# Feed-forward down projection as seven block products, in a two-layer Conformer trunk on one core

## The chip, the core and the metric

The kernel runs on one NeuronCore of a Trainium2 chip. The core has five engines with queues of their own: PE (TensorE, matrix products into PSUM), DVE (VectorE, elementwise), ACT (ScalarE, elementwise with tables), POOL (GpSimd) and SP (SyncE, which issues most DMAs). Each engine runs its own list of instructions strictly in order, and waits on semaphores for the others. The metric is the time in microseconds of one execution on the device; lower is better.

## The reference

Two layers. Each layer is a half-step feed-forward network, a mixer (a causal convolution group beside a differential attention group), and a second half-step feed-forward network. The activations are 512 positions by 1024 channels in float32, the hidden width is 2816.

```
def swiglu(h, w_gate, w_up, w_down):
    return (jax.nn.silu(h @ w_gate) * (h @ w_up)) @ w_down

for l in range(DEPTH):                                   # DEPTH = 2
    x = x + 0.5 * swiglu(rms_norm(x, ffn1_norm[l]), ffn1_w_gate[l], ffn1_w_up[l], ffn1_w_down[l])
    h = rms_norm(x, mix_norm[l])
    a, g, q, k, v = jnp.split(h @ w_in[l], splits, axis=-1)
    conv_out = conv_module(a, g, conv_w[l], conv_b[l], conv_norm[l])
    ...                                                  # q, k normed per head, lambda, diff_out
    x = x + jnp.concatenate([conv_out, diff_out], axis=-1) @ w_out[l]
    x = x + 0.5 * swiglu(rms_norm(x, ffn2_norm[l]), ffn2_w_gate[l], ffn2_w_up[l], ffn2_w_down[l])
```

## The kernel before

**Layout.** Channels lie on the 128 partitions: x is eight tiles of 128 channels by 512 positions, the hidden layer is 22 tiles ("features" below) of 128. A product is formed in three matmuls, because each float32 operand is split in two float32r parts, hi and lo: hi times hi, hi times lo, lo times hi (`mm3`). Weights are split on the fly: SP loads a raw tile, ACT copies it to hi, DVE subtracts hi from raw and gets lo (`parts_of`, L96 and L97; in the mixer POOL does the subtraction). The raw, hi and lo tiles lie in rings (`RING`): five raw, four hi and four lo of 1024 columns, and two each of 512.

**Feed-forward (`ffn`).** The 22 features are done in three parts (`PARTS`) of 6, 8 and 8. In the first part the gate and up products are plain: eight channel tiles, 512 positions wide, 48 matmuls a feature. In the two later parts gate and up of one feature are computed together by a Strassen-Winograd scheme (`seven`): the contraction is cut in two halves, the positions in two halves, and gate and up are the two block columns, so that seven block products of half width (256 positions) take the place of eight. `Halves` makes the sums of the normed activations (th, tl) that it needs; `sums` makes the sums of the weights: an accumulating DMA on POOL's queue adds u1 to two operands at once (L137), and two POOL additions make two more (L142, L143). The seven products of a feature are 84 matmuls of 128 by 256 columns (L362). The seventh product is deferred: it is issued in the next feature, behind its first two products (`before()`, `rest`), and followed by the multiplication with Silu of the gate and the split of the hidden tile into hi and lo (`gated`, L401 and L402).

After the features of a part its down product is done plainly: for each of the eight output tiles, `gather` loads the weights, and 3 matmuls a feature, 512 wide, add up in one PSUM bank (ps_d, L159, L162, L163); DVE adds half of it to x (L452). After the last part this loop also calls `after(m)`: the tile of the next norm (`Prep.tile`), or the store of the output.

**Mixer.** It starts with products of its own (`conv_in`, `project`), with the row statistics placed inside the first ones (`first_products` with `early`). The bias of the attention is made once, in the first feed-forward network (`aside`: `make_bias`, then `make_scalars`): small DMAs and a broadcast of 1280 KB in POOL's queue, and two matmuls on PE.

**Order.** The framework orders each engine's list by a cost model of its own at build time, except for matmuls that are held in program order (`keep_in_program_order`). All weight loads are on SP's queue. An instruction that waits holds whatever stands behind it on its engine.

Of the kernel before, what the change touches and what calls it, by code (L numbers as in the profile page):

```python
# [39 lines left out]
STATS_AT = 5  # L40
HS = SEQ // 2


PARTS = ((0, 6), (6, 8), (14, 8))
PLAIN = PARTS[0][1]

SPACE = 392
# [19 lines left out]
def trunk(ctx: ExitStack, tc: tile.TileContext, xt, par, lamv, relb, onehot,  # L67
# [21 lines left out]
    RING = {"wraw": 5, "whi": 4, "wlo": 4, "wraw2": 2, "whi2": 2, "wlo2": 2}  # L89

    def ring(tag, n=1024):
        dt = F32 if "raw" in tag else F32R
        return wp.tile([P, n], dt, tag=tag, name=tag, bufs=RING[tag])

    def parts_of(raw, hi, lo, eng=None):
        S.activation(hi, raw, AF.Copy)  # L96
        (eng or V).tensor_tensor(out=lo, in0=raw, in1=f32(hi), op=ALU.subtract)  # L97

    def chunk(src, eng=None):
        raw, hi, lo = ring("wraw"), ring("whi"), ring("wlo")  # L100
        nc.sync.dma_start(raw, src)
        parts_of(raw, hi, lo, eng)
        return hi, lo

    def gather(src, blocks, eng=None):

        raw, hi, lo = ring("wraw"), ring("whi"), ring("wlo")
# [8 lines left out]
        c = slice(0, len(blocks) * P)  # L116
        parts_of(raw[:, c], hi[:, c], lo[:, c], eng)
        return hi, lo

    def sums(g, u):  # L120

        h = slice(0, 512), slice(512, 1024)
        w = {}

        def give(name, t, n, raw):
            w[name] = tuple(p[:, h[n]] for p in t)
            parts_of(raw, *w[name])

        whole = ring("wraw")
        nc.sync.dma_start(whole, g)  # L130
        two = ring("wraw")
        nc.sync.dma_start(two[:, h[0]], g[:, h[0]])
        nc.sync.dma_start(two[:, h[1]], u[:, h[1]])
        u2 = ring("wraw2", 512)
        nc.sync.dma_start(u2, u[:, h[1]])

        nc.gpsimd.dma_start(  # L137
            two.rearrange("p (b c) -> p b c", b=2), u[:, h[0]].unsqueeze(1).broadcast_to([P, 2, 512]), accum_op=ALU.add
        )

        more = ring("wraw")
        G.tensor_tensor(more[:, h[0]], two[:, h[1]], whole[:, h[0]], op=ALU.add)  # L142
        G.tensor_tensor(more[:, h[1]], more[:, h[0]], whole[:, h[1]], op=ALU.add)  # L143
        t = ring("whi"), ring("wlo")
        parts_of(whole, *t)
        for n, name in enumerate(("g1", "g2")):
            w[name] = tuple(p[:, h[n]] for p in t)
        t = ring("whi"), ring("wlo")
        give("u2u1", t, 0, two[:, h[1]])
        give("g1u2u1", t, 1, more[:, h[0]])  # L150
        give("u2", (ring("whi2", 512), ring("wlo2", 512)), 0, u2)
        t = ring("whi"), ring("wlo")
        give("all", t, 0, more[:, h[1]])
        give("g1u1", t, 1, two[:, h[0]])
        return w
# [21 lines left out]
    lead = [[ring("wraw"), ring("whi"), ring("wlo")] for _ in range(4)]  # L177
    for half in range(2):
        h, kk = slice(half * 512, (half + 1) * 512), range(half * KT // 2, (half + 1) * KT // 2)
        nc.sync.dma_start(x[:, kk[0], :], xt[kk[0]])  # L180
        for n, (raw, hi, lo) in enumerate(lead):
            nc.sync.dma_start(raw[:, h], gu1[0, n // 2, n % 2][:, h])
            parts_of(raw[:, h], hi[:, h], lo[:, h])
        for k in kk[1:]:
            nc.sync.dma_start(x[:, k, :], xt[k])
    lead = [[tuple(t[1:]) for t in lead[2 * m : 2 * m + 2]] for m in range(2)]
    ident = const.tile([P, P], F32, tag="ident", name="ident")
    make_identity(nc, ident)
    ones = const.tile([P, P], F32, tag="ones", name="ones")
    G.memset(ones, 1.0)  # L190
    ones_r = const.tile([P, P + SPACE], F32R, tag="ones_r", name="ones_r")[:, :P]
    V.tensor_scalar(ones_r, ones, 1.0, None, op0=ALU.mult)
# [72 lines left out]
    def wpart(w, b, n=P):  # L265
        return w[0][:, b * n : (b + 1) * n], w[1][:, b * n : (b + 1) * n]

# [13 lines left out]
    def first_products(pr, w, ps, early=False):  # L281
# [5 lines left out]
        for k in range(KT):  # L287
            if early and k == STATS_AT:
                rc, v = rows_rstd(pr.s, DM, pin=True)
            for i in range(2):  # L290
                mm3(ps[0][i], wpart(w[0][i], k), pr[k], k == 0, k == KT - 1, pin=early and k in (0, STATS_AT))
        for i in range(2):
            for k in range(KT):
                if early and i == 0 and k == STATS_AT:
                    r = spread(rc, "rb", pin=True)
                mm3(ps[1][i], wpart(w[1][i], k), pr[k], k == 0, k == KT - 1, pin=early and k in (0, STATS_AT))
        return rc, v, r

    def pair_banks(turn):
        tag = ("sc", "po", "mm")[turn % 3]  # L300
# [3 lines left out]
    class Halves:  # L304
# [4 lines left out]
        def __init__(self, fp, pr, r):  # L309
# [4 lines left out]
            free = [(fp, tag, 1) for tag in ("hh6", "hh7", "hl6", "hl7")]  # L314
            free += [(wp, tag, 2) for tag in ("whi2", "wlo2") for _ in range(2)]
            a, b = slice(0, HS), slice(HS, SEQ)
            for j in range(KT // 2):
                for k in (j, j + KT // 2):
                    pool, tag, bufs = free.pop()
                    h = pool.tile([P, SEQ], F32, tag=tag, name="hn", bufs=bufs)  # L320
# [3 lines left out]
                t = fp.tile([P, 3, HS], F32, tag="ht", name="ht", bufs=2)  # L324
# [20 lines left out]
    def seven(halves, w, banks, fp, before, last):  # L345
# [9 lines left out]
        def go(ps, wt, xt, first=False):  # L355
# [3 lines left out]
            for j in range(KT // 2):  # L359
                (wh, wl), (xh, xl) = wpart(w[wt], j), at(j)  # L360
# [21 lines left out]
        def rest():  # L382
# [4 lines left out]
            V.scalar_tensor_tensor(us, us, -1.0, g, op0=ALU.mult, op1=ALU.mult)  # L387
            return banks[0]
# [3 lines left out]
    def ffn(pr, gu, dn, after, lead=None, aside=None):  # L392
        with tc.tile_pool(name="ffn", bufs=1) as fp:
            r = halves = None
            for m0, many in PARTS:
                hh, held, late = [], [], []

                def gated(n, us):
                    hi = fp.tile([P, SEQ], F32R, tag=f"hh{n}", name="hh")
                    lo = fp.tile([P, SEQ], F32R, tag=f"hl{n}", name="hl")  # L400
                    S.activation(hi, us, AF.Copy)  # L401
                    V.tensor_tensor(lo, us, f32(hi), op=ALU.subtract)  # L402
                    hh.append((hi, lo))

                def finish():
                    if late:
                        n, rest = late.pop()
                        gated(n, rest())

                for mm in range(many):  # L410
                    m = m0 + mm
                    if m == 4 and aside:
                        aside()
                    if m >= PLAIN:
                        w = sums(gu[m, 0], gu[m, 1])
                        late.append((mm, seven(halves, w, pair_banks(m), fp, finish, mm == many - 1)))
                        continue
                    w = lead[m] if lead and m < 2 else [chunk(gu[m, 0]), chunk(gu[m, 1])]
                    held.append((mm, w, pair_banks(m)))
                    if m == 0:  # L420
                        continue
                    if m == 1:
                        first = lead_products if lead else first_products
                        _, _, r = first(pr, [h[1] for h in held], [h[2] for h in held])
                    else:
                        for i in range(2):
                            products(pr, w, held[-1][2][i], i)
                    for n, _, ps in held:
# [6 lines left out]
                        gated(n, us)  # L435
# [3 lines left out]
                finish()  # L439
                if m0 == 0:  # L440
                    halves.settle()
                blocks = [divmod(m0 + kk, HALF) for kk in range(many)]
                blocks = [(half, m * HALF + f) for m in range(KT) for half, f in blocks]
                w = None
                for m in range(KT):
                    ps = bank("mm", "ps_d")
                    for kk in range(many):
                        b = m * many + kk
                        if b % 8 == 0:
                            w = gather(dn, blocks[b : b + 8])  # L450
                        mm3(ps, wpart(w, b % 8), hh[kk], kk == 0, kk == many - 1)
                    V.scalar_tensor_tensor(x[:, m, :], ps, 0.5, x[:, m, :], op0=ALU.mult, op1=ALU.add)  # L452
                    if m0 + many == FT:
                        after(m)


    bias = const.tile([P, HEADS, SEQ], F32, tag="bias", name="bias")

    def make_bias():
# [15 lines left out]
        nc.gpsimd.dma_start(bias, skew)  # L475
# [38 lines left out]
    def mixer(l, pr, after):  # L514
        with tc.tile_pool(name="mix", bufs=1) as mp, tc.tile_pool(name="mt", bufs=2) as mt:
            us = [None] * CT
            row = {}
            turn = iter(range(12))
# [383 lines left out]
```

## Time and profile before

| | |
|---|---|
| median of 3 runs | 1822.91 us (1822.59 to 1823.46) |
| profiled execution | 1822.3 us span, which is its own time from the first to the last instruction; the page gives no other for it |
| PE, DVE, ACT, POOL busy | 1794.2, 1201.3, 886.2, 623.2 us |
| granted TensorE clock | 0.997 of full on average |
| DMA | 227.01 MB, 125 GB/s on average |

The profile gives the busy time of each engine, groups of instructions by line, the chain of work that ended last (each step followed back to what released it), and what an engine waited for. Matmul times in it overlap their neighbours, so the distance from one start to the next is what a matmul costs. L numbers are lines of the kernel; a name such as `wlo<-wraw,whi` is output and inputs of an instruction, with buffer numbers left out; "[8.84 <-DMA lamv]" is the engine's idle time before an instruction and what ended it.

### The profile page before, as it was taken

Reading aid. Unit: us, or ns where it says so; the run is one execution under the profiler, and the core shown is the slowest. Engines: PE = TensorE matmul, PEld = TensorE weight load, DVE = VectorE, ACT = ScalarE, POOL = GpSimd, SP = SyncE. Lnnn points to the kernel's source line nnn. Section 1 sums busy time; section 2 is a strip of 40 time slices with the busy share of each in tenths; the row PEclk is TensorE's granted clock in tenths of the full one; section 3 lists DMA queues with packets and bytes.
Section 4 is the critical chain, followed back from the end, with each engine's and each line's share of the span. In section 5 each row is a group of like instructions: output and inputs, shape, how many; then the busy total and the mean of one; then the engine's idle time right before and its main releaser. Section 6 shows DMA issues by size and latency. Waiting matters only on the chain.

```text
span 1822.3 us, 27888 instructions
## 1 busy us (share of the span) xinstructions
PE 1794.2 (98%) x10692; PEld 1586.2 (87%) x10692; DVE 1201.3 (66%) x1854; ACT 886.2 (49%) x1452; POOL 623.2 (34%) x431
## 2 busy tenths in 40 slices
PE   8899999999999999999999999999999999999999
PEld 6779999888779889999888998998887888998997
DVE  6757547558876857647567574665688588574662
ACT  5536436445764436436434463554458444363551
POOL 3024024149943023124110241322698420231320
PEclk9999999999999999999999999999999999999999
DMA  6346546422213347546423564563231123564561
GB/s 225 128 99 191 150 129 178 134 92 83 81 35 94 98 105 191 149 126 184 132 90 108 133 175 132 151 185 99 77 99 64 47 94 113 134 175 133 151 173 48
DMA packets 105238, 227.01 MB, mean 125 GB/s; under 512 B 11559, under 2 KB 29238, under 8 KB 105104
## 3 DMA queue, kind: packets, MB, share of 16 engines
q1 hardware_dynamic: 85824, 188.78, 31.9%
q0 software_dynamic: 18992, 36.28, 11.6%
q8 instruction: 84, 1.38, 0.3%
q14 instruction: 50, 0.41, 0.1%
q10 hardware_dynamic: 288, 0.16, 0.0%
HBM read 223.07 MB, written 3.42 MB: 124 GB/s over the span
## 4 chain that ended last, share of the span: by engine, by line
PE 92%; DVE 4%; DMA 1%; issue 1%; ACT 1%; DVEq 0%; ACTq 0%
PE ps_pair L362 35%; PE ps_d L159 9%; PE ps_d L162 9%; PE ps_d L163 9%; PE ps_pair L163 5%; PE ps_pair L162 5%; PE ps_pair L159 5%; PE ps_pair L570 2%; PE ps_pair L569 2%; PE ps_pair L571 2%; PE ps_out L159 1%; PE ps_out L162 1%; PE ps_sc L687 1%; PE ps_out L163 1%; DMA lamv<-in_lamv 1%
## 5 line engine op out<-in xcount | busy, mean ns | idle before, releaser
L96 ACT ACTIVATE whi<-wraw 128x512 fp32r<-128x512 f32 (+1 forms) x580 | 458.8, 815 | 670.5 <-PE ps_d L162 231.4
L97 DVE TENSOR_TENSOR wlo<-wraw,whi 128x512 fp32r<-128x512 f32 (+1 forms) x536 | 509.0, 972 | 208.5 <-ACT whi L96 204.0
L362 PE MATMUL ps_pair<-acth,wlo 128*128 128x256 f32 x1024 | 289.8, 283 | 0.0
L362 PE MATMUL ps_pair<-actl,whi 128*128 128x256 f32 x1024 | 289.8, 283 | 0.0
L362 PE MATMUL ps_pair<-acth,whi 128*128 128x256 f32 x1024 | 289.7, 283 | 0.0
L159 PE MATMUL ps_d<-hh,whi 128*128 128x512 f32 x704 | 274.5, 394 | 8.9 <-DVE x L452 3.6
L162 PE MATMUL ps_d<-hl,whi 128*128 128x512 f32 x704 | 275.7, 392 | 1.5 <-DVE hl L402 1.5
L163 PE MATMUL ps_d<-hh,wlo 128*128 128x512 f32 x704 | 274.6, 391 | 0.0
L137 POOL DMA_DIRECT2D wraw<-in_gu x64 | 77.0, 1203 | 491.1 <-DMA wraw<-in_gu 197.6
L362 PE MATMUL ps_pair<-th,wlo 128*128 128x256 f32 x768 | 217.3, 283 | 0.0
L362 PE MATMUL ps_pair<-tl,whi 128*128 128x256 f32 x768 | 217.2, 283 | 0.0
L362 PE MATMUL ps_pair<-th,whi 128*128 128x256 f32 x768 | 217.2, 283 | 0.0
L159 PE MATMUL ps_pair<-acth,whi 128*128 128x512 f32 x512 | 200.6, 395 | 5.8 <-ACT whi L96 5.8
L162 PE MATMUL ps_pair<-actl,whi 128*128 128x512 f32 x512 | 201.1, 393 | 0.3
L163 PE MATMUL ps_pair<-acth,wlo 128*128 128x512 f32 x512 | 200.3, 392 | 0.7 <-DVE wlo L97 0.7
L362 PEld LDWEIGHTS ps_pair<-actl,whi 128*128 128x128 f32 x1024 | 196.6, 192 | 0.3
L362 PEld LDWEIGHTS ps_pair<-acth,whi 128*128 128x128 f32 x1024 | 196.6, 192 | 0.3
L362 PEld LDWEIGHTS ps_pair<-acth,wlo 128*128 128x128 f32 x1024 | 196.6, 192 | 0.0
L452 DVE SCALAR_TENSOR_TENSOR x<-ps_d,x 128x512 f32<-128x512 f32 x96 | 65.3, 690 | 196.0 <-PE ps_d L163 195.9
L142 POOL TENSOR_TENSOR wraw<-wraw 128x512 f32<-128x512 f32 x64 | 91.0, 1423 | 294.1 <-DMA wraw<-in_gu 253.2
L159 PEld LDWEIGHTS ps_d<-hh,whi 128*128 128x128 f32 x704 | 132.8, 189 | 42.2 <-DVE x L452 9.0
L162 PEld LDWEIGHTS ps_d<-hl,whi 128*128 128x128 f32 x704 | 132.9, 189 | 28.6 <-DVE hl L402 2.0
(173 smaller groups left out, 3311.5 us busy)
## 6 DMA issues: line engine op xcount, KB each, us to landing
wraw<-in_gu SPq DMA_DIRECT2D x108, 512.0 KB, 3.6
wraw<-in_gu SPq DMA_DIRECT2D x200, 256.0 KB, 3.7
wraw<-in_gu POOLq DMA_DIRECT2D x64, 512.0 KB, 5.5
wraw<-in_wqkv SPq DMA_DIRECT2D x24, 512.0 KB, 3.5
wraw<-in_dn SPq DMA_DIRECT2D x52, 192.0 KB, 2.9
wraw<-in_wag SPq DMA_DIRECT2D x16, 512.0 KB, 3.6
wraw<-in_wout SPq DMA_DIRECT2D x16, 512.0 KB, 3.4
wraw<-in_dn SPq DMA_DIRECT2D x24, 320.0 KB, 3.5
```

Source lines behind the costliest of these rows:

```text
L96: S.activation(hi, raw, AF.Copy)
L97: (eng or V).tensor_tensor(out=lo, in0=raw, in1=f32(hi), op=ALU.subtract)
L137: nc.gpsimd.dma_start(two.rearrange("p (b c) -> p b c", b=2), u[:, h[0]].unsqueeze(1).broadcast_to([P, 2, 512]), accum_op=ALU.add)
L142: G.tensor_tensor(more[:, h[0]], two[:, h[1]], whole[:, h[0]], op=ALU.add)
L159: first = T.matmul(ps, wh, xh, start=start, stop=False)
L162: T.matmul(ps, wh, xl, start=False, stop=False)
L163: T.matmul(ps, wl, xh, start=False, stop=stop)
L362: mm = T.matmul(ps, l, r, start=first and i == j == 0, stop=False, skip_group_check=True)
L452: V.scalar_tensor_tensor(x[:, m, :], ps, 0.5, x[:, m, :], op0=ALU.mult, op1=ALU.add)
L569: T.matmul(ps[n], xh[:, t], wh, start=k == 0, stop=False)
L570: T.matmul(ps[n], xh[:, t], wl, start=False, stop=False)
L571: T.matmul(ps[n], xl[:, t], wh, start=False, stop=k == KT - 1)
```

## The change

- Both later parts also do their down product as seven half-width block products. The part's eight features are two groups of four, the output tiles are taken in pairs m and m + 4, and each of the four pairs is one block (`seven_down`). `Hidden` makes the sums of the hidden tiles that this needs (in the buffers yh, yl), `down_sums` those of the weights. The order of the features in a part is changed so that the groups' weights lie in runs.
- The seventh product of a block is deferred into the next block, of the last block of a part into the next part, and of the last part into the first products of the next stage (`tail`, `begin`, `ORDER`); at the end of the kernel it stands alone.
- `sums` is written anew for both uses: each of the seven operands is a raw tile of 512 columns, taken in the order of use; u1 is added by separate accumulating DMAs to two of them, and the two further sums are done on DVE where POOL did them.
- All weight rings have nine tiles of 512 columns.
- `aside` calls make_scalars ahead of make_bias; the bias tile lies in the mixer's pool and is loaded from DRAM in each mixer. The last tap of the convolution writes to SBUF where an ACT copy did. `pair_banks` counts through the whole kernel. The plain down of the first part uses these banks too.

```
-PARTS = ((0, 6), (6, 8), (14, 8))
+PARTS = (
+    ((0, 1, 2, 3, 4, 5), "first"),
+    ((6, 11, 7, 12, 8, 13, 9, 14), "seven"),
+    ((10, 18, 15, 19, 16, 20, 17, 21), "last"),
+)
+ORDER = (0, 4, 1, 5, 2, 6, 3, 7)
...
-    RING = {"wraw": 5, "whi": 4, "wlo": 4, "wraw2": 2, "whi2": 2, "wlo2": 2}
+    RING = {"wraw": 9, "whi": 9, "wlo": 9}
...
+    def sums(load, n=512):
+        def get(part, dst, add=False):
+            for to, src in load(part):
+                if add:
+                    nc.gpsimd.dma_start(dst[:, to], src, accum_op=ALU.add)
+                else:
+                    nc.sync.dma_start(dst[:, to], src)
+        w = {}
+        r = {k: ring("wraw", n) for k in ("u2u1", "u2", "g1", "g2", "all", "g1u2u1", "g1u1")}
+        get("u2", r["u2u1"])
+        get("g1", r["g1u1"])
+        get("u1", r["u2u1"], True)
+        get("u2", r["u2"])
+        get("g1", r["g1"])
+        get("g2", r["g2"])
+        get("u1", r["g1u1"], True)
+        for k in ("u2u1", "u2", "g1", "g2"):
+            w[k] = parts_of(r[k])
+        V.tensor_tensor(r["g1u2u1"], r["u2u1"], r["g1"], op=ALU.add)
+        V.tensor_tensor(r["all"], r["g1u2u1"], r["g2"], op=ALU.add)
+        for k in ("all", "g1u2u1", "g1u1"):
+            w[k] = parts_of(r[k])
+        return w
...
-        G.tensor_tensor(more[:, h[0]], two[:, h[1]], whole[:, h[0]], op=ALU.add)
-        G.tensor_tensor(more[:, h[1]], more[:, h[0]], whole[:, h[1]], op=ALU.add)
...
+    def down_sums(dn, m, m2, f1, f2):
+        at = {"g1": (m, f1), "g2": (m, f2), "u1": (m2, f1), "u2": (m2, f2)}
+        return sums(lambda k: [(to, dn[half, row][:, c]) for to, half, row, c in runs(*at[k])], len(f1) * P)
...
-        for k in range(KT):
-            if early and k == STATS_AT:
+        ks = ORDER if tail else range(KT)
+        for at, k in enumerate(ks):
+            if tail and at == TAIL_AT:
+                tail()
...
+    class Hidden:
+        def add(self, mm, rest):
...
+            rest(h)
+            if not second:
+                V.tensor_tensor(h[:, b], h[:, a], h[:, b], op=ALU.subtract)
+                self.held = h
...
+            S.activation(hi, h, AF.Copy)
+            V.tensor_tensor(lo, h, f32(hi), op=ALU.subtract)
...
+                V.scalar_tensor_tensor(t[:, 0], ha[:, b], -1.0, hb[:, b], op0=ALU.mult, op1=ALU.subtract)
+                V.scalar_tensor_tensor(t[:, 1], t[:, 0], -1.0, ha[:, a], op0=ALU.mult, op1=ALU.subtract)
+                V.scalar_tensor_tensor(t[:, 2], t[:, 0], -1.0, hb[:, a], op0=ALU.mult, op1=ALU.subtract)
+                S.activation(self.th[:, :, j, :], t, AF.Copy)
+                V.tensor_tensor(self.tl[:, :, j, :], t, f32(self.th[:, :, j, :]), op=ALU.subtract)
...
+    def seven_down(hid, w, fp, m, m2, first, before):
...
+        go(c, "u2u1", "t1")
+        S.activation(keep[:, 3], c, AF.Copy)
+        if first:
+            most, rest = range(n - 1), range(n - 1, n)
+            go(a, "g1", "b11")
...
+        else:
+            go(d, "u2", "t4")
+            before()
+            go(a, "g1", "b11")
+            S.activation(keep[:, :2], banks[0].rearrange("p (n c) -> p n c", n=2), AF.Copy)
+            go(b, "g2", "b21")
+            go(c, "all", "b22")
+            go(a, "g1u2u1", "t2")
+        S.activation(keep[:, 2], a, AF.Copy)
+        two = banks[1].rearrange("p (n c) -> p n c", n=2)
+        V.tensor_tensor(two, two, keep[:, 0::2], op=ALU.add)
+        V.scalar_tensor_tensor(x[:, m, :], banks[1], 0.5, x[:, m, :], op0=ALU.mult, op1=ALU.add)
+        def finish():
+            go(a, "g1u1", "t3")
+            V.tensor_tensor(d, a, keep[:, 3], op=ALU.add)
+            V.tensor_tensor(a, a, keep[:, 1], op=ALU.add)
+            V.scalar_tensor_tensor(x[:, m2, :], banks[0], -0.5, x[:, m2, :], op0=ALU.mult, op1=ALU.add)
+        return finish
...
     def aside():
+        make_scalars()
         make_bias()
-        make_scalars()
```

More of the change, by code (lines that the diff above doesn't have):

```diff
@@ L175, in trunk @@
         nc.scalar.dma_start(pars[l], par[l])
-    lead = [[ring("wraw"), ring("whi"), ring("wlo")] for _ in range(4)]
+    lead = [[] for _ in range(4)]
     for half in range(2):
@@ L313, in __init__ @@
             self.whole = []
-            free = [(fp, tag, 1) for tag in ("hh6", "hh7", "hl6", "hl7")]
-            free += [(wp, tag, 2) for tag in ("whi2", "wlo2") for _ in range(2)]
+            four = [fp.tile([P, 4, SEQ], F32, tag=tag, name="hn") for tag in ("yh", "yl")]
+            free = [t[:, n] for t in four for n in range(4)]
             a, b = slice(0, HS), slice(HS, SEQ)
@@ L386, in rest @@
             us = banks[0].rearrange("p (n c) -> p n c", n=2)
-            V.scalar_tensor_tensor(us, us, -1.0, g, op0=ALU.mult, op1=ALU.mult)
-            return banks[0]
-        return rest
[L392 to L411, printed above, removed]
+            to = us if out is None else out.rearrange("p (n c) -> p n c", n=2)
@@ new lines, in seven_down, with go @@
+    def seven_down(hid, w, fp, m, m2, first, before):
+        banks = pair_banks()
+        a, d = banks[0][:, :HS], banks[0][:, HS:]
+        b, c = banks[1][:, :HS], banks[1][:, HS:]
+        n = hid.n
+        keep = fp.tile([P, 4, HS], F32, tag="gn", name="keep", bufs=2)
+        begun = set()
+        def go(ps, wt, xt, js=range(n)):
+            at = hid.get(xt)
+            side = 0 if ps is a or ps is d else 1
+            wh, wl = w[wt]
+            for i, j in enumerate(js):
+                f = slice(j * P, (j + 1) * P)
+                xh, xl = at(j)
+                for l, (s, r) in enumerate(((wh, xh), (wh, xl), (wl, xh))):
+                    mm = T.matmul(ps, s[:, f], r, start=side not in begun, stop=False, skip_group_check=True)
+                    begun.add(side)
+                    if i == l == 0:
+                        tc.keep_in_program_order(mm)
+        go(c, "u2u1", "t1")
[3 more added lines that the diff above has]
+            go(a, "g1", "b11")
+            S.activation(keep[:, 0], a, AF.Copy)
+            go(b, "g2", "b21", most)
+            go(c, "all", "b22", most)
+            go(d, "u2", "t4", most)
+            go(a, "g1u2u1", "t2", most)
+            go(b, "g2", "b21", rest)
+            go(c, "all", "b22", rest)
+            go(d, "u2", "t4", rest)
+            S.activation(keep[:, 1], d, AF.Copy)
+            go(a, "g1u2u1", "t2", rest)
+        else:
[16 more added lines that the diff above has]
+        return finish
@@ new lines, in begin, with ffn, finish @@
+    def begin(pr, loads, tail=None):
+        ws = [[chunk(src) for src in pair] for pair in loads]
+        ps = [pair_banks() for _ in loads]
+        return [*zip(ws, ps)], first_products(pr, ws, ps, early=tail is not None, tail=tail)
+    def ffn(fp, pr, gu, dn, after, begun, then, aside=None):
+        halves = None
+        late = []
+        def finish():
+            if late:
+                late.pop()()
+        for fs, kind in PARTS:
+            many = len(fs)
+            hh, held = [], []
+            if kind == "first":
+                for mm, m in enumerate(fs):
@@ L412, in ffn @@
                     if m == 4 and aside:
                         aside()
[L414 to L421, printed above, removed]
@@ L474, in make_bias @@
         skew = bass.AP(d2.tensor, d2.offset + P - 1, [[RLEN - 1, P], [P * RLEN, HEADS], [1, SEQ]])
-        nc.gpsimd.dma_start(bias, skew)
+        table.append(skew)
     nlam, gq, gsub, ghalf = [], [], [], []
@@ L562, in project @@
                 js = (2 * pair, 2 * pair + 1)
-                ps = pair_banks(next(turn))
+                ps = pair_banks()
                 for k in range(KT):
```

260 lines of the change are left out of this document (155 added, 105 removed).

## The prediction

> **What bounds the kernel now.** I read the page's span, engine table and chain shares first, then the chain that ended last in order of time, then stretches of the timeline.
>
> ```profile
> span 1822.3 us, 27888 instructions
> PE 1794.2 (98%) x10692; PEld 1586.2 (87%) x10692; DVE 1201.3 (66%) x1854; ACT 886.2 (49%) x1452; POOL 623.2 (34%) x431
> PE 92%; DVE 4%; DMA 1%; issue 1%; ACT 1%; DVEq 0%; ACTq 0%
> ```
>
> PE is 98% busy and 92% of the chain. A busy PE only says that matmuls overlap, so I take their price from start to start, in the chain in order of time (start, length, what):
>
> ```profile
> 125.45 76.31 PE ps_pair L362 x636
> ...
> 250.31 76.31 PE ps_pair L362 x636
> ...
> 797.42 76.31 PE ps_pair L362 x636
> ...
> 1021.76 76.31 PE ps_pair L362 x636
> ```
>
> Each row opens an eight-feature part. 636 half-width matmuls take 76.31 us: 0.120 us each. The part from 125.45 to 250.31 is 124.86 us long; its seven-product up side is 8 x 84 x 0.120 = 80.64 us, so its plain down, 192 full-width matmuls, is 44.22 us: 0.2303 each. Inside a part PE waits for nothing of weight. From 797.42 to 1021.76 lie one part and the next FFN's first six features: those cost 224.34 - 124.86 = 99.48 us when PE is fed. The very first FFN is not fed. The chain there, then DVE's timeline, then busy times by stretch (last columns: granted clock, DMA share, GB/s):
>
> ```profile
> 31.16 0.44 PE ps_rows L210 x4
> 43.02 0.96 PE ps_bias L469 x2
> 44.27 2.25 DMA oneh<-in_onehot
> 46.65 0.38 PE ps_bias L469 x2
> 57.96 16.54 DMA lamv<-in_lamv
> ...
> 74.53 0.23 DVE L485 TENSOR_TENSOR lamp<-lamv 128x64 f32<-128x64 f32 x1 [8.84 <-DMA lamv<-in_lamv]
> ...
> 40.00:50.00 10.00, 7.32 (x26) 4.76 (x25) 6.55 (x10) 4.09 (x5) 1.63 (x3) 0.87 0.32 107
> 80.00:90.00 10.00, 6.55 (x22) 4.78 (x20) 10.00 (x19) 8.09 (x14) 0.00 (x0) 0.83 0.40 133
> ```
>
> After the lead's two features (end 31.6) come four features and the down, 336 of 432 matmuls: 77.4 of the 99.48 us, and 1.4 us of bias matmuls. PE could reach the first seven-product feature at 110.4; it does at 125.45, so 15.0 us are lost. DVE stands 8.84 us before lamv and then works through 80 to 90 without a gap, while PE starts 22 matmuls where 43 would fit, at a granted clock of 0.83.
>
> **The change, part by part.**
>
> *The down as seven products.* Per part, 192 full-width matmuls become 4 blocks x 7 products x 12 = 336 half-width ones: 336 x 0.120 = 40.32 us instead of 44.22, 3.90 less. Eight parts: **-31.2**, all of it on PE's path.
>
> [...]
>
> *Its cover on DVE.* What hides below PE is now nearly as long as PE. Timeline and chain:
>
> ```profile
> 151.95 1.29 DVE L97 TENSOR_TENSOR wlo<-wraw,whi 128x512 fp32r<-128x512 f32 x2 [0.62 <-ACT whi L96]
> 153.16 0.69 DVE L402 TENSOR_TENSOR hl<-ps_pair,hh 128x512 fp32r<-128x512 f32 x1
> ...
> 83.50 0.67 DVE ht L327 x2
> ...
> 88.39 0.87 DVE tl L330
> ```
>
> A 512-wide operation takes 0.605 us from start to start (two from 151.95 to 153.16), 256 wide 0.33, 768 wide 0.87. An up feature will need 7 wlo, 2 operand sums (they were POOL's, L142 and L143), the Silu sum, the last product and hl: 12 x 0.605 = 7.26; two 256-wide sums, 0.66; and for the down's operand combinations 0.33 in one feature, 3 x 0.33 + 0.87 in the next, 1.10 on average. That is 9.02 us beside PE's 84 x 0.120 = 10.08. A down block needs 12 operations of 512 and two of 256, 7.92, and 9.13 in the last part with two tiles of the next norm. So it costs 0, covered by PE with 1 us to spare; what it costs without that cover is rival 1. ACT gains th and some copies, about 7 us of 10.
>
> *Its cover in the loads.* The down now brings seven operands of 256 KB per block, as the up side does, whose stretches run at 180 GB/s and a DMA share of 0.68, against 128 and 0.54 in a plain down. I add nothing for bandwidth, but the order is tight. DVE's sum for feature f+1 stands ahead of feature f's conversions of the same operand. It waits for a loop through four queues: DVE frees a slot, SP loads u2 into it, POOL's DMA adds u1, DVE sums, DVE converts and so frees the next slot. Behind the waiting sum on DVE are conversions for PE and the updates that free PSUM and keep; behind the slot wait on SP are the feature's other loads, behind POOL's wait the second accumulate.
>
> ```profile
> 160.00:180.00 20.00, 20.00 (x169) 20.00 (x168) 14.50 (x22) 12.45 (x22) 10.20 (x7) 1.00 0.68 180
> 220.00:240.00 20.00, 20.00 (x90) 16.57 (x89) 6.87 (x8) 3.95 (x5) 5.83 (x4) 1.00 0.54 128
> ...
> wraw<-in_gu SPq DMA_DIRECT2D x200, 256.0 KB, 3.7
> wraw<-in_gu POOLq DMA_DIRECT2D x64, 512.0 KB, 5.5
> wraw<-in_dn SPq DMA_DIRECT2D x28, 256.0 KB, 2.7
> q0 software_dynamic: 18992, 36.28, 11.6%
> ```
>
> POOL's one DMA of 512 KB becomes two of 256 KB, a size the trace lacks on that queue. A packet of queue 0 costs 0.116 x 16 x 1822.3 / 18992 = 0.178 us; 128 packets fewer over 16 engines save 1.4 us: 4.1 us, between half the row (2.75) and all of it (5.5). The load takes 2.7 to 3.7; loads are now spread out, so 3.1. With some 0.4 us of wakes the chain is 5.9 to 9.6 and I take 7.6; with the sum and the conversion the loop turns in 8.8 us, under 10.08. Down blocks cut an operand into up to three runs, three POOL DMAs and 7 to 11 SP loads; that can lengthen a turn by a microsecond or two, but DVE's order runs about eight products (11.5 us) ahead of PE, and gains 1 us a feature. Cost 0, both ends kept for rival 2.
>
> *The first down block of a part* needs the last feature's th and tl. PE lays 66 matmuls, 7.9 us, over a chain of two 256-wide sums, the product, three wlo, three combinations, hl, one operand sum, ACT's th and DVE's tl: 0.66 + 0.605 + 1.82 + 0.99 + 0.605 + 0.605 + 0.83 + 0.87 = 7.0, with wakes 7.4. The operand sum may wait for its load: 0 to 1 us, eight times, **+4**.
>
> ```profile
> L329 ACT ACTIVATE th<-ht 128x768 fp32r<-128x768 f32 x16 | 12.9, 833 | 1.4 <-DVE ht L328 1.4
> 1818.61 0.69 DVE x L452
> ```
>
> *The deferred last product.* At three stage ends it moves behind two steps of the next stage's products; then x[7], its norm tile and the row sums follow. PE has 5.5 us of steps over some 3 us of DVE and ACT work, but DVE also converts eight new halves there: 0 to 2 us each, **+3**. At the kernel's end two 256-wide sums and an update follow the last product where the one update at 1818.61 did: **+1**.
>
> *The start.* make_scalars now precedes make_bias, so lamv leaves POOL's queue before the 1280 KB broadcast that it stood behind. The one-hot table is issued later (about 56 us by DVE's order), but PE's bias matmul has moved back by 75 matmuls as well, to about 60. Of the 15.0 us I take 12 back, bounds 0 and 15, because DVE then has its work done before PE's down needs the last feature: **-12**. In exchange the second feature's accumulate stands behind the broadcast in POOL's queue:
>
> ```profile
> 55.23 1.15 POOL L473 DMA_DIRECT2D d<-d  x1 [1.28 <-DMA d<-brow]
> 74.64 0.77 POOL L475 DMA_DIRECT2D bias<-d  x1 [16.09 <-DMA d<-d]
> ```
>
> 19 us from issue to end; issued near 73 it ends near 92, and PE wants that feature after 110: 0.
>
> *Rings of 512, bias loaded in each mixer, the conv's copy dropped.* The bias has 100 us until the first softmax: 0. POOL converts 88 halves where it did 44 wholes:
>
> ```profile
> L97 POOL TENSOR_TENSOR wlo<-wraw,whi 128x1024 fp32r<-128x1024 f32 x44 | 105.6, 2405 | 48.1 <-ACT whi L96 48.0
> L641 POOL TENSOR_TENSOR yp<-yp,prod 128x512 f32<-128x512 f32 x78 | 101.0, 1295 | 6.1 <-ACT prod L640 3.5
> 432.00:442.00 10.00, 10.00 (x47) 8.30 (x46) 8.10 (x13) 4.91 (x8) 10.00 (x5) 1.00 0.56 178
> ```
>
> At 1.295 us a half for 1.203, that is 4 us a layer on a POOL that is full here; PE has other work, only the mixer's end waits for yp. Both layers -2 to +8, **+2**.
>
> Sum: -31.2 - 12 + 4 + 3 + 1 + 2 = -33.2 on the profiled 1822.3: 1789.1. The median of the runs is 0.6 above that span, so 1790.
>
> **The rivals.**
>
> 1. *DVE becomes the bound.* If an operation holds DVE for its whole busy time, an up feature is 12 x 0.69 + 2 x 0.43 + (4 x 0.43 + 0.95)/2 = 10.5 us, 0.4 over PE; 64 features, +25: 1815.
>
> ```profile
> 158.60 0.43 DVE L384 TENSOR_TENSOR ps_pair<-ps_pair,keep 128x256 f32<-128x256 f32 x1 [0.20 <-PE ps_pair L362]
> L330 DVE TENSOR_TENSOR tl<-ht,th 128x768 fp32r<-128x768 f32 x16 | 15.0, 954 | 0.0
> ```
>
> Against it: pairs 0.605 apart. For it: DVE now waits for loads, ACT and PE in one strict order with 1 us of room.
>
> [...]
>
> 2. *Slower: the accumulate loop.* If 256 KB lands no sooner than 512 KB, the chain is 9.6 and the loop 10.8 us, 0.73 over PE in each of 96 features and blocks: +70, 1860. It decides from a loop of 10.42 us: (1823 - 1790)/96 above 10.08. For it: a sum that waits holds the conversions behind it. Against it: the packet price.
>
> 3. *The start isn't mended:* DVE is still late for its own work: 1802.
>
> **How the numbers follow.** Forecast 0.57 (its own range 1776 to 1802), rival 1 0.15, rival 2 0.14, rival 3 0.10, other ways 0.04. The range 1772 to 1818 leaves out rival 2 and the other ways. 0.2% (3.6 us) is about what a measurement of this kernel can tell from no change: faster holds all but rival 2 and a longer rival 1, 0.83; same 0.03; slower 0.14.
>
> **What would show it.** Right: parts 121 us apart, 84 half-width matmuls every 10.08 us in up and down alike, the first of them near 112, no lamv on the chain. Wrong: PE idle before whi or wlo with DVE full (rival 1); DVE idle before the sums on wraw with a wraw DMA as releaser, a feature taking over 10.08 us (rival 2); a granted clock under 1 inside a part.

## The result, and the profile after

The changed kernel takes 1974.6 us (1971.3 to 1976.4, four runs), the kernel before 1823.2 (1822.6 to 1824.3) beside it: a ratio of 1.083, 95% interval 1.081 to 1.084. It is 151 us slower where 33 us faster was forecast. The profiled execution has a span of 1973.0 us. From the page of the changed kernel:

```profile
PE 1835.3 (93%) x11844; PEld 1674.6 (85%) x11844; DVE 1483.2 (75%) x2603; ACT 1028.8 (52%) x1930; POOL 554.2 (28%) x523
...
PE 65%; DMA 14%; DVE 11%; issue 5%; ACT 4%; POOL 0%; DVEq 0%; SPq 0%; ACTq 0%; POOLq 0%
```

PE held 92% of the chain before and holds 65% now; DMA went from 1% to 14% and DVE from 4% to 11%. DVE is busy for 75% only, so it is not full: something makes it wait. The waits of the changed kernel, DVE's longest (us in total, times, longest):

```profile
DVE wraw L160 <- DMA wraw<-in_gu: 148.0, 57, 4.4
DVE wraw L160 <- DMA wraw<-in_dn: 78.8, 30, 4.3
```

L160 is the sum g1u2u1, one in each of the 96 features and blocks; 87 of them wait for their accumulated operand, 2.6 us each on average.

Where the time lies is told by the eight parts with seven products, cut at their first matmul. The stretches of the changed kernel (length, busy time of PE, PEld, DVE, ACT and POOL, granted clock, DMA share, GB/s), one part and the sum of all eight, then the sum of the kernel before:

```profile
1682.53:1818.69 136.16, 125.49 (x997) 123.91 (x996) 102.82 (x180) 74.27 (x139) 21.08 (x24) 0.96 0.64 157
...
sum 1139.85, PE 1031.27 PEld 1013.61 DVE 847.55 ACT 602.46 POOL 208.19; mean PE 128.91 PEld 126.70 DVE 105.94 ACT 75.31 POOL 26.02
```

```profile
sum 998.90, PE 996.22 PEld 932.40 DVE 612.71 ACT 483.36 POOL 276.07; mean PE 124.53 PEld 116.55 DVE 76.59 ACT 60.42 POOL 34.51
```

The parts take 141 us more. The first of them starts 15.7 us earlier (chain of the changed kernel, against 125.45 before):

```profile
109.73 28.69 PE ps_pair L385 x239
```

The remaining 25 us (150.7 + 15.7 - 141.0) lie in the mixers, at stage ends and in first parts.

One turn of the loop, from the timeline of the changed kernel. The rows of four engines are put in order of time:

```profile
150.22 0.69 DVE L160 TENSOR_TENSOR wraw<-wraw 128x512 f32<-128x512 f32 x1 [1.24 <-DMA wraw<-in_gu]
...
151.54 0.33 SPq L147 DMA_DIRECT2D wraw<-in_gu  x1
...
160.79 0.69 DVE L160 TENSOR_TENSOR wraw<-wraw 128x512 f32<-128x512 f32 x1 [2.73 <-DMA wraw<-in_gu]
...
163.54 0.69 DVE L101 TENSOR_TENSOR wlo<-wraw,whi 128x512 fp32r<-128x512 f32 x1
...
164.26 0.33 SPq L147 DMA_DIRECT2D wraw<-in_gu  x1
...
167.35 0.86 POOL L145 DMA_DIRECT2D wraw<-in_gu  x1 [10.13 <-DMA wraw<-in_gu]
...
174.26 0.69 DVE L160 TENSOR_TENSOR wraw<-wraw 128x512 f32<-128x512 f32 x1 [3.02 <-DMA wraw<-in_gu]
...
177.40 0.58 PE L385 MATMUL ps_pair<-th,whi 128*128 128x256 f32 x1 [3.33 <-ACT keep L399]
```

The sum starts at 160.79; the conversion that frees the slot (163.54) ends 3.44 later, and SP's load starts at once; the accumulate is issued 3.09 behind that; the next sum starts 6.91 behind the accumulate. That is 13.47 us. In the turn before it the load starts 1.32 behind the sum (150.22 to 151.54) and the turn is 10.57. PE needs 10.08 for a feature, so even the short turn is too long. It stands at last (177.40), and then matmuls cost more than before, as the clock in the stretches shows:

```profile
172.00:174.00 2.00, 2.00 (x18) 1.87 (x16) 0.00 (x0) 0.00 (x0) 0.00 (x0) 1.00 0.90 195
174.00:176.00 2.00, 0.07 (x1) 0.00 (x0) 1.74 (x4) 0.07 (x1) 0.00 (x0) 1.00 0.13 25
176.00:178.00 2.00, 0.60 (x3) 0.60 (x4) 2.00 (x4) 2.00 (x5) 0.00 (x0) 0.61 0.39 131
178.00:180.00 2.00, 2.00 (x11) 2.00 (x11) 2.00 (x4) 1.26 (x3) 0.86 (x1) 0.50 0.62 193
```

After a wait of 3.3 us the granted clock is 0.50, and in 2 us 11 matmuls are under way instead of 18. PE's last matmul ends at 174.07. In stretches of 0.2 us the clock is 1.00 up to 176.40, 0.61 from there to 176.60 and 0.50 behind that: here it fell some 2.4 us into the wait. The same rows show the DMA engines at a share of 0.90, then 0.13: SP issues the five loads of a feature close together, from 164.26 on, and then the DMA engines have little to do until DVE has summed and freed slots again.

The accumulate's price is in the page's list of DMA issues (number, size, median us from issue to landing) and in the longer list of the same view:

```profile
wraw<-in_gu POOLq DMA_DIRECT2D x128, 256.0 KB, 5.9
...
wraw<-in_dn POOLq DMA_DIRECT2D x48, 64.0 KB, 5.4
```

At 512 KB it was 5.5 before. By these medians half the size, and an eighth of it, lands no sooner. Whether that is the price of the size is asked in experiments 4 and 5.

### The profile page after: what moved, and what is told of

The parts are those of the page before. It is cut to its first block, busy times and chain, and to the rows that moved or that the text cites. A ratio compares the mean times of both kernels' runs of the same rounds, so it can differ in the third digit from the quotient of the medians.

```text
span 1973.0 us, 33085 instructions
## 1 busy us (share of the span) xinstructions
PE 1835.3 (93%) x11844; PEld 1674.6 (85%) x11844; DVE 1483.2 (75%) x2603; ACT 1028.8 (52%) x1930; POOL 554.2 (28%) x523
## 4 chain that ended last, share of the span: by engine, by line
PE 65%; DMA 14%; DVE 11%; issue 5%; ACT 4%; POOL 0%; DVEq 0%; SPq 0%; ACTq 0%; POOLq 0%
PE ps_pair L385 16%; PE ps_pair L470 11%; DMA wraw<-in_gu 10%; PE ps_pair L181 8%; PE ps_pair L180 8%; PE ps_pair L177 8%; DMA wraw<-in_dn 4%; DVE wlo L101 4%; ACT whi L100 2%; PE ps_sc L824 2%; PE ps_out L177 2%; PE ps_out L180 2%; PE ps_out L181 2%; PE ps_pair L709 1%; PE ps_pair L707 1%
## 5 line engine op out<-in xcount | busy, mean ns | idle before, releaser
L100 ACT ACTIVATE whi<-wraw 128x512 fp32r<-128x512 f32 x928 | 572.7, 627 | 527.2 <-PE ps_pair L180 190.2
L101 DVE TENSOR_TENSOR wlo<-wraw,whi 128x512 fp32r<-128x512 f32 x840 | 588.1, 715 | 102.4 <-ACT whi L100 91.5
L145 POOL DMA_DIRECT2D wraw<-in_gu x128 | 111.6, 874 | 819.6 <-DVE wlo L101 413.4
L160 DVE TENSOR_TENSOR wraw<-wraw 128x512 f32<-128x512 f32 x96 | 66.5, 692 | 227.1 <-DMA wraw<-in_gu 148.0
L385 PEld LDWEIGHTS ps_pair<-th,whi 128*128 128x128 f32 x768 | 152.4, 198 | 66.7 <-ACT keep L399 60.8
L145 POOL DMA_DIRECT2D wraw<-in_dn x112 | 99.3, 1263 | 301.7 <-DVE wlo L101 78.5
L470 PE MATMUL ps_pair<-hl,whi 128*128 128x256 f32 x512 | 155.0, 303 | 14.9 <-DVE hl L435 14.8
L470 PE MATMUL ps_pair<-hh,whi 128*128 128x256 f32 x512 | 154.5, 302 | 11.1 <-ACT hh L434 11.1
L470 PE MATMUL ps_pair<-hh,wlo 128*128 128x256 f32 x512 | 153.7, 300 | 0.0
L385 PEld LDWEIGHTS ps_pair<-th,wlo 128*128 128x128 f32 x768 | 153.4, 200 | 0.0
```

The lines of the kernel that those rows point to most:

```text
L145: nc.gpsimd.dma_start(dst[:, to], src, accum_op=ALU.add)
L160: V.tensor_tensor(r["g1u2u1"], r["u2u1"], r["g1"], op=ALU.add)
L385: mm = T.matmul(ps, l, r, start=first and i == j == 0, stop=False, skip_group_check=True)
L470: mm = T.matmul(ps, s[:, f], r, start=side not in begun, stop=False, skip_group_check=True)
```

## The experiments

The theory after this reading: the loop slot, load, accumulate, sum, conversion, slot sets the pace of the eight parts. Its rivals: the transfers do not fit into 10.08 us (throughput), or DVE's own work does not.

**1. A ring of their own for the accumulated operands.**

```
-    RING = {"wraw": 9, "whi": 9, "wlo": 9}
+    RING = {"wraw": 7, "wacc": 4, "whi": 8, "wlo": 8}
...
-        r = {k: ring("wraw", n) for k in ("u2u1", "u2", ...)}
+        r = {k: ring("wacc" if k in ("u2u1", "g1u1") else "wraw", n) for k in ("u2u1", "u2", ...)}
```

Plain chunks take turns between the two rings. The sizes add up to 27 tiles, as in the changed kernel.

> The two accumulated operands get a ring of their own (four tiles), the other five of a feature one of seven; hi and lo have eight each. Nothing else. By the order of the instructions the load of u2u1 is then released some 22 DVE operations (over 13 us) ahead of the sum that reads it, and six ahead of the previous sum, where in the changed kernel it is released 12 ahead and one to five behind the previous sum. Loop theory (slot, load, accumulate, sum, conversion, slot again; 10.6 to 13.5 us a turn): the chain of about 10 us now lies beside the turn before, DVE's waits ahead of its first sum go, features come back to about 10.1 us, the eight parts to about 122 us: 1974 less 8 x 22 = about 1800 (1790 to 1825). Throughput theory (five loads and two accumulates of 256 KB do not fit into 10.08 us): it stays at 1950 to 1975. DVE theory (DVE's own work with its waits for ACT fills a feature): no change, 1970.

Measured: 1806.5 us (1804.8 to 1809.9), ratio to before 0.9911 (0.9894 to 0.9927). Its one long wait of the sum (at 90.19, ahead of the eight parts), the sum of its eight parts (each 121.1 to 121.2 us long, at a clock of 1.00) and its accumulates:

```profile
DVE wraw L162 <- DMA wacc<-in_gu: 7.6, 1, 7.6
```

```profile
sum 969.22, PE 959.12 PEld 955.25 DVE 858.71 ACT 614.14 POOL 213.42; mean PE 119.89 PEld 119.41 DVE 107.34 ACT 76.77 POOL 26.68
```

```profile
wacc<-in_gu POOLq DMA_DIRECT2D x128, 256.0 KB, 4.7
```

With the same instructions of DVE and the same bytes the parts come from 1139.9 to 969.2 us. Loop theory holds; throughput and DVE fall, since by either of them the time had to stay. The 170.6 us are 98.5 less idle PE (108.6 to 10.1) and 72.2 less busy PE for the same matmuls. The second figure goes with the lowered clock (0.93 to 0.96 in the changed kernel's parts); how much of it is only the modelled end of a matmul ahead of each wait is open. The accumulate also lands 1.2 us sooner by the median. That the stall had slowed it is not shown: in experiment 6 the parts take little longer than here, and it lands in 5.9 again.

**2. The slot released later.** The same edit with other sizes.

```
-    RING = {"wraw": 9, "whi": 9, "wlo": 9}
+    RING = {"wraw": 6, "wacc": 3, "whi": 9, "wlo": 9}
```

> The same kind of edit in the other direction: own ring of three for the two accumulated operands, six for the others, 9 and 9 for hi and lo. As many tiles as before, but the load of u2u1 is now released four to eight DVE operations behind the previous sum, two to three more than in the changed kernel. Loop theory: each turn is 2 to 3 x 0.6 = 1.2 to 1.8 us longer, in 96 features and blocks: 1974 + 115 to 175 = 2090 to 2150. Throughput and DVE theories: no change, 1965 to 1985.

Measured: 1998.4 us (one run), 24 more than the changed kernel. The direction is that of the loop, the size is not. Its timeline:

```profile
158.98 0.69 DVE L162 TENSOR_TENSOR wraw<-wacc,wraw 128x512 f32<-128x512 f32 x1 [3.23 <-DMA wacc<-in_gu]
...
161.85 0.33 SPq L149 DMA_DIRECT2D wacc<-in_gu  x1
...
171.07 0.69 DVE L162 TENSOR_TENSOR wraw<-wacc,wraw 128x512 f32<-128x512 f32 x1 [3.26 <-DMA wacc<-in_gu]
```

A short turn went from 10.57 to 12.09, its DVE leg from 1.32 to 2.87, as expected. The long turn that follows did not grow: the load starts at 175.20, the accumulate at 178.54 and the next sum at 184.51, 13.44 us behind the sum at 171.07. Its DVE leg went from 3.44 to 4.13, but from the accumulate's issue to the sum it took 5.97 where the changed kernel took 6.91. By the median the accumulates landed in 5.3 us here. I had added the later slot to every turn and taken the rest of the turn as fixed.

**3. Without the accumulates.**

```
-                if add:
-                    nc.gpsimd.dma_start(dst[:, to], src, accum_op=ALU.add)
-                else:
+                if not add:
```

> The changed kernel without the two accumulating DMAs: u1 is left out of two operands of each feature and block, so a part of the computation is missing, and 54 - 3 MB of transfers in POOL's queue with it. Loop theory: the turn loses 5.9 to 6.6 us of accumulate and a wake of 0.6, about 5.5 to 6.5 us are left, under PE's 10.08, and the sums wait no more: about 1795 (1785 to 1815). Throughput theory: two of seven transfers fewer, also about 1800. DVE theory: 1960 to 1975.

Measured: 1825.3 us (one run), above the expected 1785 to 1815. 149 of the 168 us that the loop costs go with the accumulate. It is still 19 us above the kernel with the own ring. Some 8 of these lie in the eight parts (977 against 969 us) and the rest mostly in the mixers, where two operations of the attention that experiment 8 is about last 6.0 and 6.2 us, against 4.4 and 0.17 with the own ring.

**4. and 5. The price of an accumulate by its size**, measured on the kernel before.

```
-        nc.gpsimd.dma_start(two..., u[:, h[0]].unsqueeze(1).broadcast_to([P, 2, 512]), accum_op=ALU.add)
+        for n in (1, 0):
+            nc.gpsimd.dma_start(two[:, h[n]], u[:, h[0]], accum_op=ALU.add)
```

> The kernel before with its one accumulate of 512 KB (a broadcast to two operands) cut in two accumulates of 256 KB, u2u1 first; the rest as before. It measures the price of an accumulate by its size where the queue is not pressed. By the packet price taken in the prediction each lands in 4.1 us; if the price is a latency that the size hardly changes, in 5 to 6. The time stays within 1815 to 1835 in either case, since the sums are on POOL and have room there.

The second kernel does the same with four slices of 256 columns.

> The kernel before with its accumulate of 512 KB cut in four of 128 KB. For the price by size: 512 KB landed in 5.5 us, two of 256 KB in 5.2 each. If the price is mostly a latency: 4.3 to 5.2 at 128 KB; if it goes by packets: 2 to 3. Time 1820 to 1840 (two more issues of some 0.9 us a feature on a POOL with room).

Measured: 1823.4 us with two of 256 KB, 1917.7 with four of 128 KB (one run each). The medians from issue to landing are 5.5, 5.2 and 5.1 us at 512, 256 and 128 KB, which looks like a latency that the size hardly changes. It is not: the medians mix DMAs that stand behind one another in POOL's queue. The rows of single issues in one feature say so, the first and the second of two, then the first and the last of four:

```profile
wraw<-in_gu POOLq DMA_DIRECT2D x1, 256.0 KB, 4.1
...
wraw<-in_gu POOLq DMA_DIRECT2D x1, 256.0 KB, 5.7
```

```profile
wraw<-in_gu POOLq DMA_DIRECT2D x1, 128.0 KB, 3.0
...
wraw<-in_gu POOLq DMA_DIRECT2D x1, 128.0 KB, 8.3
```

Over all 64 features the first of two lands in 4.0 us at the median and the first of four in 3.0. So the price does go by the size here where nothing of the same queue is ahead, and 256 KB costs the 4.1 us that the prediction took. The 5.9 of the changed kernel is not the price of the size alone. For the second kernel 1820 to 1840 was expected, which misses by far. POOL's timeline tells why:

```profile
165.42 1.27 POOL L143 TENSOR_TENSOR wraw<-wraw 128x512 f32<-128x512 f32 x1 [6.73 <-DMA wraw<-in_gu]
166.77 1.62 POOL L144 TENSOR_TENSOR wraw<-wraw 128x512 f32<-128x512 f32 x1
168.32 3.48 POOL L140 DMA_DIRECT2D wraw<-in_gu  x4
```

POOL issues four (3.48), waits for the last (6.73) and sums (2.9): 13.1 us in this feature, in order, whatever its busy share. The kernel before had such a turn too, and it fitted into 10.08 with one issue of 1.2.

**6. The sums back on POOL**, in the changed kernel with its rings.

```
-        V.tensor_tensor(r["g1u2u1"], r["u2u1"], r["g1"], op=ALU.add)
-        V.tensor_tensor(r["all"], r["g1u2u1"], r["g2"], op=ALU.add)
+        G.tensor_tensor(r["g1u2u1"], r["u2u1"], r["g1"], op=ALU.add)
+        G.tensor_tensor(r["all"], r["g1u2u1"], r["g2"], op=ALU.add)
```

> The changed kernel with its two operand sums (g1u2u1 and all) back on POOL, as before the change; rings as changed. DVE then waits for no accumulate of its own, so a late sum no longer holds the conversion of the feature before, and the loop spans two features (sum, conversion, slot, load, accumulate, next sum but one). Loop theory, the DVE's place in it being what makes it one turn a feature: the parts come back to 121 to 124 us, total 1800 to 1825. If the nine common slots are too few whoever does the sums: it stays over 1900. POOL's sums took 1.3 to 2.3 us before, 2.9 to 4 a feature with 1.8 of issuing, so POOL is not full.

Measured: 1821.5 us (1811.8 to 1826.5), ratio to before 0.998 (0.996 to 1.000). Its first part:

```profile
110.14:231.73 121.59, 120.06 (x997) 119.66 (x996) 106.34 (x159) 75.02 (x139) 61.56 (x48) 1.00 0.74 176
```

Nine common slots are nearly enough if the waiting sum does not stand in DVE's list ahead of the conversion that frees the slot. So two things together made the turn one of each feature: the slot and the queue that the sum waits in. Either one mended takes the stall away, the ring wholly and this edit nearly so: the eight parts take some 981 us here, 121.5 to 124.7 each, against 969 with the own ring, and the total is 15 us above that kernel's.

**7. The start alone**, on the kernel before.

```
     def aside():
+        make_scalars()
         make_bias()
-        make_scalars()
```

> The kernel before with one edit: make_scalars ahead of make_bias. The prediction's term for it was -12 (0 to -15); in the changed kernel the first seven-product feature starts at 109.6 instead of 125.3. If that gain belongs to the start and nothing else hangs on it: 1823 - 11 to 16 = 1807 to 1812. If the second accumulate behind the broadcast costs it (the part I put at 0): 1815 to 1823.

Measured: 1813.2 us (1812.7 to 1815.4), ratio 0.9947 (0.9932 to 0.9961), 10.9 us less. That is 1 us outside the first of the two expected ranges, and nearer to it than to the second. The first seven-product feature starts at 113.5, 11.8 us earlier than before, where the changed kernel starts it at 109.6; so about 4 us of the changed kernel's earlier start come from other edits. The DMA issues of this kernel, then of the kernel before, say how: lamv lands in 3.6 us, where it took 10.0 behind other work of that queue.

```profile
lamv<-in_lamv POOLq DMA_DIRECT2D x2, 128.0 KB, 3.6
```

```profile
lamv<-in_lamv POOLq DMA_DIRECT2D x2, 128.0 KB, 10.0
```

**8. A small operation of the attention on POOL.**

```
-                V.scalar_tensor_tensor(se, sums[i][:, 0, :], VD * EPS, sums[i][:, 0, :], op0=ALU.mult, op1=ALU.mult)
+                G.tensor_tensor(se, sums[i][:, 0, :], sums[i][:, 0, :], op=ALU.mult)
+                G.tensor_scalar(se, se, VD * EPS, None, op0=ALU.mult)
```

> The changed kernel with one small operation of the attention (se, 128x4) on POOL, in two instructions, where DVE did it. In the changed kernel two of its eight instances last 6.0 and 6.2 us instead of 0.15, and DVE has nothing done meanwhile. If they are held by POOL's back-to-back work and the attention waits for DVE there: 8 to 12 us less, 1962 to 1967. If other work covers it, or another operation is held in its place: 1972 to 1976.

Measured: 1973.4 us (1969.5 to 1974.5), no change that can be told. By PE's rows the two mixers, each with the first part behind it, are 14.5 us shorter together, about what the two long operations (6.00 and 6.21) had cost, but DVE's waits ahead of its sums are 13 us longer over the eight parts. Why the loop waits more with this edit is open.

**9. and 10. The best version, and its down product undone.** The own ring with se on POOL; then the same with a plain down product in the later parts (192 full-width matmuls a part), of which the core is

```
-                w = down_sums(dn, m, m2, f1, f2)
-                rest = seven_down(hid, w, fp, m, m2, m == 0, finish)
+                for kk in range(many):
+                    b = m * many + kk
+                    if b % 4 == 0:
+                        w = [gather(dn, blocks[b : b + 4])]
+                    mm3(ps, wpart(w, b % 4), hh[kk], kk == 0, kk == many - 1)
```

> The kernel with the own ring for the accumulated operands, and se of the attention on POOL. On the changed kernel this edit took the two 6 us holds of DVE away and shortened the two mixers by 14.5 us together, but the parts with their loop gave it back. Here no part waits in the loop, and one se lasts 4.4 us, the others under 0.8: 1806.5 - 4.4 = 1802 (1799 to 1805) if the hold costs what it lasts; 1806 if it is covered.

> The same kernel with the down product of both later parts undone: plain, 512 wide, as in the first part, the rest as it is (loop removed, start mended, se on POOL). If the seven products are worth the prediction's 3.9 us a part (or the 3.7 that a part shows): eight parts, +29 to +31 less 5 for the last product deferred at stage ends, the kernel's end and the first down block's waits: 24 to 31 above the other kernel of this call, near 1830. If the second use of the scheme is worth nothing because its loads and sums cost what its products save: within 5 us of it.

Measured: 1804.6 us (1800.5 to 1805.7), ratio to before 0.9896 (0.9880 to 0.9913), the lowest median of all; and 1813.9 (1813.1 to 1815.8), ratio 0.9947 (0.9932 to 0.9962). Whether se on POOL gained anything beside the own ring can't be told: 1804.6 lies between the two expected values, and its runs overlap those of the own ring alone. One part of each, from the stretches, the seven products first:

```profile
1001.41:1122.57 121.16, 120.03 (x998) 119.61 (x996) 106.37 (x183) 74.92 (x139) 22.61 (x26) 1.00 0.76 178
```

```profile
1007.20:1131.42 124.22, 124.22 (x865) 116.67 (x864) 83.31 (x136) 61.00 (x113) 13.87 (x16) 1.00 0.63 153
```

The down as seven products is worth 9.4 us by the medians, 12.3 between the profiled executions (1811.0 and 1798.7), where 24 to 31 was expected. The next section says where the rest goes.

## Why the prediction was wrong

**What bounds the kernel.** The reading of before held: matmuls of 0.120 us in a fed PE, and 15 us to be had at the start.

**The down as seven products, -31.2.** Right in kind. A pair of parts has 2004 matmuls of the new kind between its first matmul and the next stage (12 stand behind that), 240.48 us at 0.120, and takes 2 x 121.16 = 242.32. But the plain down beside it costs 124.22 - 80.64 = 43.6 us, 0.227 a matmul, not the 44.2 of the kernel before: 8 x (43.6 - 40.3) = -26.

**Its cover on DVE.** Right. In the kernel with the own ring DVE was busy for 107.3 of 121.2 us in a part, 89% as in the sum (9.02 of 10.08), and the sum no longer waited. Rival 1 is not seen: pairs stay some 0.6 us apart (160.79 and 161.40 in the changed kernel, 0.69 busy each).

**Its cover in the loads.** This is the step that failed: "the loop turns in 8.8 us, under 10.08 ... Cost 0". The loop, its four queues and what stands behind the waiting sum were as described; two terms were too small. The accumulate was taken as 4.1 us from a price by packets, between bounds of 2.75 and 5.5; it lands in 5.9 in the changed kernel, above the upper bound. The price itself was right: 4.1 is what 256 KB takes at the head of its queue in experiment 4. What the step left out is that it would not land alone. The DMA engines' share was 0.85 while the accumulate shown above was under way, and 0.58 while the one of 4.1 was; that the other transfers slow it is likely by these figures, but no run changes them alone, so the cause of the longer accumulate stays open. And DVE's leg, from the sum to the freed slot, was two operations, 1.2 us; in the longer of the two turns shown four more operations stand between, and it is 3.44. The load, taken as 3.1, is 3.01 and 3.09. Added up the two turns are 10.57 and 13.47 us, not 8.8.

**Rival 2** named this mechanism with 14% and a loop of 10.8 us, +70: the right sign, under half the size. Its condition, 256 KB landing no sooner than 512 KB, came true in the changed kernel, though not because of the size. What it left out is DVE's longer leg, an accumulate above the upper bound, and the clock, 0.50 behind PE's wait of 3.3 us above and 0.93 to 0.96 over the parts.

**The first down block, +4.** The waits of four pairs are 4 x (242.32 - 240.48) = 7.4 us. The term that is missing is ACT's copy of a partial product, for which PE waits once in each part, in the first down block (best version):

```profile
PE ps_pair L472 <- ACT keep L490: 7.0, 8, 0.9
```

**Stage ends +3, kernel's end +1.** The down gains 26 - 7.4 = 18.7 us inside the parts and 12.3 in all, so the ends cost about 6, or 9 if the 9.4 of the medians is taken. That is what is left over; no run measures the ends alone.

**The start, -12.** Right: 10.9 alone, by the medians.

**Mixer and rings, +2.** Too small in the changed kernel. The two long instances of se told of below, 6.00 and 6.21 us, are 12 us of it. Without them, without the loop and with a plain down, the kernel stands 10.1 us below before by the medians (1813.9 to 1824.0), where the start alone gave 10.9, so rings, bias and the convolution's copy together cost about 1 us where 2 were taken, a difference that runs of this scatter hardly tell.

Without the loop the change measures 1806.5, with se on POOL too 1804.6: 17 and 15 us above the forecast, and inside its range. The other 168 us are the loop.

## What to carry to other kernels

Before an operation is moved to an engine, follow the slot that its operand comes from: if the instruction that frees it stands behind the waiting one in the same list, load, transfer and conversion add up to one turn per step (10.57 and 13.47 us here, over the 10.08 of PE), and busy shares do not show it (DVE 75%). A DMA's price in a quiet queue need not hold beside other transfers: the 256 KB that landed in 4.1 us there took 5.9 beside the loads of the changed kernel, so keep a loop's sum clear of its limit by more than that. And where DMAs are issued behind one another, look at the first of them; the median over all hides the price of one (5.2 us for 4.0 at 256 KB). A ring of their own for the few operands with a long way took 168 us off here in the same space.

## What the runs showed of the hardware

An accumulating DMA with nothing of its queue ahead of it landed in 3.0, 4.0 and 5.5 us at 128, 256 and 512 KB (medians over the first of four, the first of two and the only one of a feature). Those issued right behind another landed later: the second 256 KB of the feature shown took 5.7 where the first took 4.1, the fourth 128 KB 8.3 where the first took 3.0. Between kernels it differs as much: at 256 KB the medians are 5.9 in the changed kernel and with the sums on POOL, 5.3 with the later slot, 4.7 with the own ring.

A small DVE operation of 0.15 us took 6.00 in one place, where POOL worked on without a gap. From the timeline of the changed kernel, DVE and then POOL:

```profile
520.36 6.00 DVE L861 SCALAR_TENSOR_TENSOR se<-sums 128x4 f32<-128x4 f32 x1
...
522.62 1.29 POOL L779 TENSOR_TENSOR yp<-yp,prod 128x512 f32<-128x512 f32 x1
523.84 1.29 POOL L101 TENSOR_TENSOR wlo<-wraw,whi 128x512 fp32r<-128x512 f32 x1
525.06 1.29 POOL L779 TENSOR_TENSOR yp<-yp,prod 128x512 f32<-128x512 f32 x1
```

Of its eight instances another lasts 6.21 us, the other six 0.15 to 0.97. POOL runs without a gap until 526.35, five of its instructions long beside se, and se ends at 526.36; the other long one ends at 1504.63, and POOL's work without a gap at 1504.60. That POOL held se is my inference from these times; no run changes POOL's work there alone. In the kernel before no se lasted longer than 0.16, but POOL stood idle at six of the eight. The other two came in just where one POOL instruction gave way to the next (497.65 and 1393.95, POOL's next instruction at 497.75 and 1394.04), and took 0.16 each though POOL made no pause; so what decides it is open.
